# Layer norms applied behind the projections: a two-layer decoder step on one core

## The chip, the cores and the metric

The kernel runs on one core of a Trainium2 chip. The metric is the device time of one execution in microseconds. TensorE (PE) multiplies and writes its sums to PSUM; VectorE (DVE), ScalarE (ACT) and GpSimd (POOL) do the rest; each engine works off its own queue of instructions in order. SyncE (SP) only issues transfers. All arithmetic is float32: for the large products each operand is cut into two float32r parts.

## The reference, cut to what matters

The program is one inference step of a decoder with two layers, for 256 prompt tokens and 8 x 8 sample tokens (320 token columns), 2048 features, and a feed forward part 5504 wide:

```
for layer in (0, 1):
    x = LN(alpha * x + mixer(x))          # gamma, beta of ln_g[l, 0], ln_b[l, 0]
    x = LN(alpha * x + conv_ffn(x))       # gamma, beta of ln_g[l, 1], ln_b[l, 1]

conv_ffn(h):  gate, up = split(h @ w_up)
              out = (silu(causal_conv3(gate) + bias) * up) @ w_down
LN(x) = (x - mean) * rsqrt(var + eps) * gamma + beta     # over the 2048 features
```

There are four layer norms. After layer 0 the normalised x also feeds the keys and values (w_kv) and queries (w_q) of layer 1. The outputs are the last x, the new keys and values, and the last two gate rows of each sequence.

## The kernel before, in words

Activations are kept transposed: features on partitions, in 16 tiles of 128, and the 320 tokens on the free axis. `Stream` (L45) carries all weights, in chunks of up to 128 x 1024: SP loads a chunk (three buffers), ACT copies it to its high part (L82) and DVE subtracts for the low part (L84) into one of three `hl` buffers, and for each 128 x 128 tile of it PE does three matmuls over the 320 token columns (L123 to L125: high by high, high by low, low by high). A `Job` is one or more blocks of 256 columns of a weight matrix. When its sums are complete, `job.epi` takes them out of PSUM; `acc` has four buffers, a block needs two.

Everything else is a generator in `Lanes`, stepped after each half of a chunk. The tile framework then orders each engine's queue by its own estimate of when an operation is ready, program order being the priority; where `tc.keep_in_program_order` stands, the order is held.

`R` holds the residual stream. `epi_wo` and `epi_down` add products to it; with the last product of a tile, `ln_tile` adds to the sums `s1` (DVE) and `s2` (squares by ACT, sums by POOL). After the last tile `ln_end` has PE sum `s1` and `s2` over the partitions and DVE, ACT and PE turn these into mean and deviation (`ln_finish`, `spread`); `normalise` then takes POOL, DVE, ACT, ACT, DVE for each of the 16 tiles to make `xh` and `xl`, the two parts of the next projection's moving operand. The order is the same at three places, which this text calls A (after the mixer of layer 0, before its `up` jobs), B (after the feed forward of layer 0, before `kvb`) and C (after the mixer of layer 1). The fourth norm makes the output and has a path of its own (`out_end`).

`big` is a pool of four buffers for the arrays of 16 tiles. `ffn_consts` transposes gamma and beta into `lnp` and the conv's constants into `stc`; it starts as a lane at the fourth `wo` job. `gen_tables_b` (L592) builds a table for layer 1 on POOL; its lane is added when the feed forward of layer 0 begins, and in the profile it ran during the `wo` jobs ahead of A.

Of the kernel before, what the change touches and what calls it, by code (L numbers as in the profile page):

```python
# [18 lines left out]
NT = NPR + NSM  # L19
DM = 2048  # L20
KD = DM // 128
# [23 lines left out]
class Stream:  # L45
    """Weights in chunks: loaded, split into two float32r parts, multiplied, ahead of one another."""
# [57 lines left out]
    def run(self, job, steps, upto=None):  # L104
        """The job's chunks, all or those before upto; steps() after each half of one."""
        nc = self.nc
        accs = job.accs
        while self.done < (job.last if upto is None else job.first + upto):
# [8 lines left out]
            for (c, cw), acc in zip(tiles, accs[i]):  # L117
                for k in range(nk):
                    xh, xl = job.mv(k0 + k)
                    o = k * w + c  # L120
                    st, sp = k0 + k == 0, k0 + k == job.nk - 1
                    hi, lo = hl[:, 0, o:o + cw], hl[:, 1, o:o + cw]
                    nc.tensor.matmul(acc[:cw, :NT], hi, xh, start=st, stop=False)  # L123
                    nc.tensor.matmul(acc[:cw, :NT], hi, xl, start=False, stop=False)  # L124
                    nc.tensor.matmul(acc[:cw, :NT], lo, xh, start=False, stop=sp)  # L125
                    if self.fine and k == 1:
                        steps()
# [8 lines left out]
class Job:  # L136
    def __init__(self, w, cols, nk, mv, epi, k0=0, kc=4, on_pool=0):
        self.on_pool, self.accs = on_pool, {}
# [28 lines left out]
# the output's twelve chunks: 1 where ACT and Pool do the step, 0 where DVE does  # L167
# [9 lines left out]
def tile_yoco(  # L177
# [22 lines left out]
    def big(name, dt=F):  # L200
        return big_p.tile([128, 5120], dt, name=name, tag="big")
# [4 lines left out]
    def cols3(t):  # L206
        return t.rearrange("p (k n) -> p k n", n=NT)
# [27 lines left out]
    S = {"sel2": sel.rearrange("p j h q -> p j (h q)")}  # L235
    st = Stream(tc, raw_p, hl_p, acc_p, 3, 3)
# [8 lines left out]
    def mv_o(k):  # L245
        return S["oh"][:, k, :], S["ol"][:, k, :]
# [24 lines left out]
    def ffn_jobs(l):  # L271
        Wu, Wd = wview(ffn_w_up[l]), wview(ffn_w_down[l])

        def up(f0, n, wide):
            cols = []
            for a in range(0, n, 2):
                w = 128 * min(2, n - a)
                cols += [(128 * (f0 + a), w), (DFF + 128 * (f0 + a), w)]
            if wide:
                job(("up", l, f0, "w"), Wu, cols[:2], KD, mv_x, lambda i, t, f0=f0: epi_up(l, f0, i, t))  # L280
            for a in range(2 if wide else 0, len(cols), 2):
                for i in range(2):
                    job(("up", l, f0, a + i), Wu, [cols[a + i]], KD, mv_x,
                        lambda _, t, f=f0 + a, i=i: epi_up(l, f, i, t))
# [11 lines left out]
        for g, (f0, n) in enumerate(starts):  # L296
            if g == 0:
                up(f0, n, True)
            else:
                up(f0, 2, False)  # L300
                down(g - 1, *starts[g - 1])
                up(f0 + 2, n - 2, False)
# [11 lines left out]
    job("kvb", W_kv, [(0, 256), (256, 256)], KD, mv_x, lambda i, t: epi_kv("kb", i, t))  # L314
    for j in range(2):
        job(("vb", j), W_kv, [(512 + 256 * j, 256)], KD, mv_x, lambda i, t, j=j: epi_kv("vb", j, t))
    for hp in range(8):
        for g in range(3):
            job(("qb", hp, g), W_q, [(2048 * g + 256 * hp, 256)], KD, mv_x,
                lambda i, t, hp=hp, g=g: epi_qb(hp, g, t))  # L320
# [7 lines left out]
    def ln_prepare():  # L328
        """R becomes ALPHA * R less, for each token, the mean of its first 128 features."""
# [12 lines left out]

    def ln_tile(d):
        """The sums for one finished 128-feature tile of R."""
# [10 lines left out]
    def ln_end():  # L355
        """The last two tiles, and the means over all: tokens on partitions, 128 of them in each column."""
# [22 lines left out]
    def ln_finish(which, mode):  # L379
        """R becomes the normalised x; mode "xs" also stores it."""  # L380
        R, L, tk = S["R"], S["fp"], S["tk"]
        m, v, rs = tk[:, 0:3], tk[:, 4:7], tk[:, 8:11]

        def spread(x, name):
            """A column of tokens in each of three, to all partitions of a row."""
            p = ps(name)
            for t, n in TG:
                i = te.matmul(p[:, 128 * t:128 * t + n], x[:n, t:t + 1].to_broadcast([n, 128]), idf[:n, :n],
                              start=True, stop=True)
                tc.keep_in_program_order(i)  # L390
            o = L.tile([128, NT], F, name=name, tag=name)
            se.activation(out=o, in_=p[:, :NT], func=AF.Copy)
            return p[:, :NT], o

        pm, m1 = spread(m, "m1")
        ve.scalar_tensor_tensor(v, m, -1.0, m, OP.mult, OP.mult)
        ve.tensor_add(rs, S["pv"][:, 0:3], v)
        se.activation(out=rs, in_=rs, func=AF.Sqrt, bias=epst)
        ve.reciprocal(rs, rs)
        pr, rstd = spread(rs, "rstd")  # L400
        S["xh"] = cols3(big("xh", FR))
        S["xl"] = cols3(big("xl", FR))

        def normalise(d):
            r = R[:, d, :]
            if d < 2:
                ve.tensor_sub(r, r, pm)
            else:
                ge.tensor_sub(r, r, m1)
# [1305 lines left out]
```

## Time and profile before

| | |
|---|---|
| device time, median of 3 runs | 3329.16 us (3326.53 to 3330.91) |
| span of the profiled execution | 3326.8 us, 2.4 us below the median |
| PE busy | 3241.7 us, 97% |
| DVE, ACT, POOL busy | 1831.1, 1364.1, 625.1 us |
| mean granted TensorE clock | 0.982 of full |

The span runs from the first to the last instruction of one profiled execution; the device time contains it. Busy PE counts matmuls in flight, so it also counts matmuls that run at the lower clock.

### The profile page before, as it was taken

Reading aid. Unit: us, or ns where it says so; the run is one execution under the profiler, and the core shown is the slowest. Engines: PE = TensorE matmul, PEld = TensorE weight load, DVE = VectorE, ACT = ScalarE, POOL = GpSimd, SP = SyncE. Lnnn points to the kernel's source line nnn. Section 1 sums busy time; section 2 is a strip of 40 time slices with the busy share of each in tenths; the row PEclk is TensorE's granted clock in tenths of the full one; section 3 lists DMA queues with packets and bytes.
Section 4 is the critical chain, followed back from the end, with each engine's and each line's share of the span. In section 5 each row is a group of like instructions: output and inputs, shape, how many; then the busy total and the mean of one; then the engine's idle time right before and its main releaser. Section 6 shows DMA issues by size and latency. Waiting matters only on the chain.

```text
span 3326.8 us, 58327 instructions
## 1 busy us (share of the span) xinstructions
PE 3241.7 (97%) x23574; PEld 3053.7 (92%) x23574; DVE 1831.1 (55%) x3169; ACT 1364.1 (41%) x2209; POOL 625.1 (19%) x820
## 2 busy tenths in 40 slices
PE   9999999999999999999999999999999999999998
PEld 7789655989999999999899898878999999999998
DVE  5747644676555555555644444555665555555556
ACT  4643444344333333333544343343443333333333
POOL 2223543451000000000401111111210000000003
PEclk8999999989999999999899999999899999999998
DMA  6655787635444444444475767766354444444444
GB/s 187 148 187 152 251 295 282 165 113 156 149 152 148 151 152 148 152 149 149 133 247 157 216 186 206 209 196 182 103 157 151 148 152 149 150 153 147 151 151 139
DMA packets 543249, 562.75 MB, mean 169 GB/s; under 512 B 24598, under 2 KB 520926, under 8 KB 538806
## 3 DMA queue, kind: packets, MB, share of 16 engines
q1 hardware_dynamic: 520692, 468.87, 46.7%
q0 software_dynamic: 19856, 85.75, 7.6%
q10 hardware_dynamic: 2432, 4.40, 0.4%
q8 instruction: 186, 3.05, 0.4%
q14 instruction: 83, 0.68, 0.1%
HBM read 542.14 MB, written 17.59 MB: 168 GB/s over the span
## 4 chain that ended last, share of the span: by engine, by line
PE 90%; DVE 4%; DMA 3%; ACT 1%; issue 1%; POOL 0%; SPq 0%; DVEq 0%; ACTq 0%; POOLq 0%
PE acc L123 26%; PE acc L124 26%; PE acc L125 26%; PE kt L1258 1%; PE acc L1076 1%; DMA vtb<-in_cache_v_b_dram 1%; PE oa L1127 1%; PE s L1055 1%; PE s L1211 1%; PE s L1051 1%; DMA kx<-in_cache_kidx_a_dram,i 1%; PE s L1158 1%; PE ob L1301 1%; DVE R L410 1%; DVE hl L84 1%
## 5 line engine op out<-in xcount | busy, mean ns | idle before, releaser
L84 DVE TENSOR_TENSOR hl<-raw,hl 128x1024 fp32r<-128x1024 f32 (+1 forms) x752 | 928.3, 1235 | 870.5 <-ACT hl L82 867.0
L82 ACT ACTIVATE hl<-raw 128x1024 fp32r<-128x1024 f32 (+3 forms) x770 | 804.2, 1045 | 1314.6 <-PE acc L125 1112.6
L123 PE MATMUL acc<-xh,hl 128*128 128x320 f32 (+1 forms) x4176 | 1315.5, 315 | 6.6 <-ACT xh L412 5.1
L124 PE MATMUL acc<-xl,hl 128*128 128x320 f32 (+1 forms) x4176 | 1298.6, 311 | 7.2 <-DVE xl L414 7.2
L125 PE MATMUL acc<-xh,hl 128*128 128x320 f32 (+1 forms) x4176 | 1296.7, 311 | 1.5 <-POOL hl L84 1.1
L123 PEld LDWEIGHTS acc<-xh,hl 128*128 128x128 f32 (+1 forms) x4176 | 789.3, 189 | 31.1 <-issue 20.2
L124 PEld LDWEIGHTS acc<-xl,hl 128*128 128x128 f32 (+1 forms) x4176 | 788.5, 189 | 15.4 <-DVE xl L414 12.6
L125 PEld LDWEIGHTS acc<-xh,hl 128*128 128x128 f32 (+1 forms) x4176 | 788.0, 189 | 6.1 <-issue 3.5
L124 PE MATMUL acc<-H,hl 128*128 128x320 f32 x1376 | 425.4, 309 | 1.1 <-POOL H L568 1.1
L123 PE MATMUL acc<-H,hl 128*128 128x320 f32 x1376 | 426.0, 310 | 0.0
L125 PE MATMUL acc<-H,hl 128*128 128x320 f32 x1376 | 425.3, 309 | 0.3 <-DVE hl L84 0.3
L124 PEld LDWEIGHTS acc<-H,hl 128*128 128x128 f32 x1376 | 258.3, 188 | 1.6 <-POOL H L568 1.6
L125 PEld LDWEIGHTS acc<-H,hl 128*128 128x128 f32 x1376 | 258.3, 188 | 0.6 <-DVE hl L84 0.6
L123 PEld LDWEIGHTS acc<-H,hl 128*128 128x128 f32 x1376 | 258.2, 188 | 0.1
L586 DVE TENSOR_TENSOR R<-R,acc 128x320 f32<-128x320 f32 x352 | 169.7, 483 | 122.1 <-PE acc L125 121.8
L551 POOL COPY gl<-E 128x2 f32<-128x2 f32 x86 | 24.8, 288 | 1039.1 <-ACT E L547 1039.1
L568 POOL TENSOR_TENSOR H<-h,H 128x320 fp32r<-128x320 f32 x86 | 106.1, 1235 | 452.8 <-ACT H L567 438.6
L123 PE MATMUL acc<-oh,hl 128*128 128x320 f32 x512 | 161.9, 317 | 0.5 <-ACT oh L992 0.5
L124 PE MATMUL acc<-ol,hl 128*128 128x320 f32 x512 | 160.6, 314 | 0.9 <-DVE ol L993 0.9
L125 PE MATMUL acc<-oh,hl 128*128 128x320 f32 x512 | 160.3, 313 | 0.0
L1148 POOL TENSOR_TENSOR bm<-tt,pmb 128x256 f32<-128x256 f32 x48 | 45.4, 971 | 324.7 <-DVE mxb L941 309.4
L123 PEld LDWEIGHTS acc<-oh,hl 128*128 128x128 f32 x512 | 97.0, 190 | 2.8 <-ACT oh L992 1.2
(390 smaller groups left out, 3191.4 us busy)
## 6 DMA issues: line engine op xcount, KB each, us to landing
raw<-in_ffn_w_up_dram SPq DMA_DIRECT2D x336, 512.0 KB, 3.6
raw<-in_ffn_w_down_dram SPq DMA_DIRECT2D x160, 512.0 KB, 3.6
raw<-in_b_w_q_dram SPq DMA_DIRECT2D x96, 512.0 KB, 3.6
raw<-in_a_w_in_dram SPq DMA_DIRECT2D x64, 512.0 KB, 4.8
krb<-in_cache_k_b_dram SPq DMA_DIRECT2D x96, 256.0 KB, 3.6
vtb<-in_cache_v_b_dram SPq DMA_DIRECT2D x92, 256.0 KB, 5.6
raw<-in_a_w_o_dram SPq DMA_DIRECT2D x32, 512.0 KB, 4.3
raw<-in_b_w_o_dram SPq DMA_DIRECT2D x32, 512.0 KB, 5.0
```

What stands on the lines that cost most here:

```text
L82: a = self.nc.scalar.activation(out=hl[:, 0, :m], in_=raw[:, :m], func=AF.Copy)
L84: b = eng.tensor_sub(hl[:, 1, :m], raw[:, :m], hl[:, 0, :m].bitcast(F))
L123: nc.tensor.matmul(acc[:cw, :NT], hi, xh, start=st, stop=False)
L124: nc.tensor.matmul(acc[:cw, :NT], hi, xl, start=False, stop=False)
L125: nc.tensor.matmul(acc[:cw, :NT], lo, xh, start=False, stop=sp)
L410: ve.scalar_tensor_tensor(r, r, lnp[:, d, which:which + 1], pr if d < 2 else rstd, OP.mult, OP.mult)
L568: ge.tensor_sub(lo, h, hi.bitcast(F))
L586: ve.tensor_add(r, r, acc[:, :NT])
L1051: te.matmul(pv[:, :, 64 * hh:64 * hh + 64], S["sel2"][:, 8 * hh + b, :], S["ms"][:, 0:1024].rearrange("p (a t) -> p a t", t=16)[:, :, 4 * ...
L1055: te.matmul(p[32 * g:32 * g + 32, :], S["qsf"][:, b, 32 * g:32 * g + 32], kts[g], start=False, stop=True, tile_position=(0, 32 * g))
L1076: te.transpose(p[:, 128 * i:128 * i + 128], kr[:, o:o + 128], idf)
L1148: ge.tensor_add(bm[:, g, :], tt, S["pmb"][:, g, :])
```

## The change

At A, B and C the product is no longer taken with the normalised x. `epi_wo` and `epi_down` form gamma times the unnormalised row at once, in two parts: `scale_hi` (ACT) and `scale_lo` (DVE), into `rh` and `rl`. Two columns are added to each row, gamma and beta (`scale_gb`), so that a matmul moves 322 columns (`NX`) in all jobs whose operand is x: 172 blocks of 128 outputs in the two feed forwards and 56 in `kvb`, `vb` and `qb`. The extra columns give u = W gamma and v = W beta. `ln_stats` finds minus the mean and the inverse deviation meanwhile (`mr`). `fix` forms (acc + u * (-mean)) * rstd when a product leaves PSUM: one small ACT copy and two DVE operations of 320 columns for each block; v comes in as the bias or scalar of the operation behind it. `ln_rest` normalises R itself afterwards (POOL, DVE, ACT), since the residual is still needed.

At A and C `rl` takes the place of `ol`, the low part of the operand that the last `wo` job still reads: `gen_lo` writes it behind that job's chunks. The first part of `ffn_consts` (gamma and beta) now runs ahead of the first `wo` job of `mixer_end`. `gen_tables_b` is added at the first `down` job. The first `up` job is no longer two blocks wide.

```diff
@@ Stream.run
-                    nc.tensor.matmul(acc[:cw, :NT], hi, xh, start=st, stop=False)
+                    nx = job.nx
+                    nc.tensor.matmul(acc[:cw, :nx], hi, xh, start=st, stop=False)
...
+    def scale_hi(d):
+        se.activation(out=S["rh"][:, d, 0:NT], in_=S["R"][:, d, :], func=AF.Identity,
+                      scale=lnp[:, d, S["which"]:S["which"] + 1])
+    def scale_lo(d):
+        ve.scalar_tensor_tensor(S["rl"][:, d, 0:NT], S["R"][:, d, :], lnp[:, d, S["which"]:S["which"] + 1],
+                                S["rh"][:, d, 0:NT].bitcast(F), OP.mult, OP.subtract)
...
+    def ln_stats(mode=None):
+        yield
+        yield
...
+        for p, x in ((pm, S["s1"]), (pv, S["s2"])):
+            for t, n in TG:
+                te.matmul(p[:n, t:t + 1], x[:, 128 * t:128 * t + n], ones_d[:, 0:1], start=True, stop=True)
...
+        yield
+        yield
+        for k, x in enumerate((m, rs)):
+            p = ps("mr")
+            for t, n in TG:
+                te.matmul(p[:, 128 * t:128 * t + n], x[:n, t:t + 1].to_broadcast([n, 128]), idf[:n, :n],
+                          start=True, stop=True)
+            se.activation(out=S["mr"][:, k, :], in_=p[:, :NT], func=AF.Copy)
+        if mode:
+            S["norm"] = lanes.add(ln_rest(mode), 1.6)
...
+    def ln_rest(mode):
...
+            ge.tensor_add(r, r, S["mr"][:, 0, :])
+            ve.scalar_tensor_tensor(r, r, lnp[:, d, w:w + 1], S["mr"][:, 1, :], OP.mult, OP.mult)
+            se.activation(out=r, in_=r, func=AF.Identity, bias=lnp[:, d, 2 + w:3 + w])
...
+    def fix(acc, t):
+        if S["stats"] in lanes.lanes:
+            lanes.drain(S["stats"])
+        uv = const.tile([128, 2], F, name="uv", tag="uv", bufs=8)
+        se.activation(out=uv, in_=acc[:, NT:NX], func=AF.Copy)
+        ve.scalar_tensor_tensor(t, S["mr"][:, 0, :], uv[:, 0:1], acc[:, :NT], OP.mult, OP.add)
+        ve.tensor_mul(t, t, S["mr"][:, 1, :])
+        return uv[:, 1:2]
...
+    def gen_lo():
+        for d in range(0, KD, 4):
+            yield
+            if d == 12:
+                yield
+            scale_gb(d, 4)
+            for i in range(4):
+                scale_lo(d + i)
+            yield
@@ epi_wo
             ve.tensor_add(r, r, acc[:, :NT])
+            scale_hi(d)
@@ epi_up
+            x = Fp.tile([128, NT], F, name="fx", tag="fx", bufs=4)
+            v = fix(acc, x)
...
-                se.activation(out=e[:, 2:258], in_=acc[:, 0:256], func=AF.Copy)
+                se.activation(out=e[:, 2:258], in_=xp, func=AF.Identity, bias=v)
...
-                ve.tensor_mul(h[:, 0:256], c[:, 0:256], acc[:, 0:256])
+                ve.scalar_tensor_tensor(h[:, 0:256], xp, v, c[:, 0:256], OP.add, OP.mult)
@@ epi_down
+        if last and not l and p == 0:
+            S["which"] = 1
+            S["rh"], S["rl"] = cols3(big("rh", FR), NX), cols3(big("rl", FR), NX)
+            scale_gb(0, KD)
...
             ve.tensor_add(r, r, acc[:, :NT])
+            if last and not l:
+                scale_hi(d)
+                scale_lo(d)
@@ ffn
+        S["stats"] = lanes.add(ln_stats(), 1.0)
...
-        if l == 0:
-            lanes.add(gen_tables_b(), 0.5)
...
+                prep = lanes.add(chain(ln_rest("ffn"), ln_prepare()), 0.8)
+            if key[0] == "down" and key[2] == 0:
+                if prep in lanes.lanes:
+                    lanes.drain(prep)
+                if l == 0 and key[3] == 0:
+                    lanes.add(gen_tables_b(), 0.5)
@@ mixer_end
+        consts = ffn_consts(stn, lnn)
+        next(consts)
+        lanes.add(consts, 0.5)
         for p in range(8):
+            if p == 7:
+                lo = lanes.add(gen_lo(), 1.0)
             if ("wo", l, p) in jobs:
                 run(("wo", l, p))
-            if p == 3:
-                lanes.add(ffn_consts(stn, lnn), 0.5)
-        g = ln_finish(0, "ffn")
-        next(g)
-        lanes.add(g, 1.0)
+        lanes.drain(lo)
+        S["xh"], S["xl"] = S["rh"], S["rl"]
```

`epi_kv` (for `kb` and `vb`) and `epi_qb` call `fix` in the same way. The fourth norm keeps `ln_end` and `out_end`.

## Rows read from the trace of the kernel before

**Rows 1.** The page's part 1: busy time, share of the span, instructions.
```profile
span 3326.8 us, 58327 instructions
...
PE 3241.7 (97%) x23574; PEld 3053.7 (92%) x23574; DVE 1831.1 (55%) x3169; ACT 1364.1 (41%) x2209; POOL 625.1 (19%) x820
```

**Rows 2.** Waits on PE: waiting line <- releaser: total us, times, longest.
```profile
PE acc L124 <- DVE xl L414: 7.2, 6, 2.6
...
PE pm L371 <- DVE R L502: 2.6, 1, 2.6
...
PE acc L124 <- POOL H L568: 1.1, 1, 1.1
```

**Rows 3.** PE's matmuls into acc at A, B, C: stretch, length, busy (count), PEclk, DMA.
```profile
706.12:740.00 33.88, 17.05 (x82) 0.65 0.20 56
1638.95:1670.00 31.05, 18.38 (x100) 0.73 0.40 113
2373.51:2405.00 31.49, 20.65 (x104) 0.73 0.23 71
```

**Rows 4.** Timeline of PE at A: start, us, instruction, idle time before it.
```profile
720.05 1.44 PE L123 MATMUL acc<-xh,hl 128*128 128x320 f32 x4 [1.70 <-ACT xh L412]
721.28 1.27 PE L333 MATMUL shift<-R,ones_s 128*128 128x320 f32 x2
724.08 0.64 PE L124 MATMUL acc<-xl,hl 128*128 128x320 f32 x1 [1.53 <-DVE xl L414]
```

**Rows 5.** Timeline of PE at C: sums, then the spreading.
```profile
2373.95 0.81 PE L371 MATMUL pm<-ones_d,s 128*64 128x1 f32 x6
...
2376.91 1.07 PE L388 MATMUL m<-idf,tk 64*128 64x64 f32 x6
2377.91 1.63 PE L388 MATMUL rstd<-idf,tk 64*128 64x64 f32 x6
```

**Rows 6.** Timeline of PE: the first and last of 42 matmuls, 320 columns, kvb stage.
```profile
1702.18 0.31 PE L124 MATMUL acc<-xl,hl 128*128 128x320 f32 x1
...
1708.19 0.31 PE L123 MATMUL acc<-xh,hl 128*128 128x320 f32 x1
```

**Rows 7.** Timeline of PE: the first and last of eight matmuls, 256 columns, indexer.
```profile
105.49 0.28 PE L728 MATMUL is<-kitr,qh 128*128 128x256 f32 x1
...
106.31 0.28 PE L729 MATMUL is<-kitr,ql 128*128 128x256 f32 x1
```

**Rows 8.** PE's groups by line and shape: count, busy us, mean ns, idle before.
```profile
L123 PE MATMUL acc<-xh,hl 128*128 128x320 f32 x4160 | 1309.3, 315 | 5.4 <-ACT xh L412 5.1 <-issue 0.3
```

**Rows 9.** DVE by line: count, ns min/median/max.
```profile
L586 DVE TENSOR_TENSOR R<-R,acc x352: 471/481/489, 800.7 to 3300.3; 128x320 f32<-128x320 f32 x176
...
L410 DVE SCALAR_TENSOR_TENSOR R<-R,lnp,rstd x48: 537/546/1235, 718.9 to 2403.5; 128x320 f32<-128x320 f32 x48
```

**Rows 10.** All engines, last down group before B: length, PE, PEld, DVE, ACT, POOL.
```profile
1612.00:1640.00 28.00, 28.00 (x196) 27.87 (x194) 25.00 (x42) 14.61 (x26) 15.81 (x13) 1.00 0.56 173
```

**Rows 11.** POOL at 630 us and at C: table's load and user, then gamma's load.
```profile
630.24 0.50 POOL L600 DMA_DIRECT2D mk<-in_c_smaskb_dram  x1
...
634.06 1.08 POOL L602 TENSOR_TENSOR sb<-trb,mk 16x512 f32<-16x512 f32 x1 [1.08 <-DMA mk<-in_c_smaskb_dram]
...
2277.89 0.50 POOL L515 DMA_DIRECT2D lnn<-in_ln_b_dram  x1
```

**Rows 12.** Timeline of DVE: first sum of the mixer of layer 1.
```profile
2277.92 0.49 DVE L502 TENSOR_TENSOR R<-R,acc 128x320 f32<-128x320 f32 x1 [2.06 <-PE acc L125]
```

**Rows 13.** All engines in the feed forward of layer 0, columns as in rows 10.
```profile
800.00:900.00 100.00, 100.00 (x684) 100.00 (x683) 55.08 (x76) 38.30 (x51) 8.45 (x17) 1.00 0.50 154
```

**Rows 14.** POOL's work on the table sb: stretch, length, busy (count), PEclk, DMA.
```profile
610.00:715.00 105.00, 53.51 (x40) 0.97 0.51 153
```

**Rows 15.** Timeline of DVE: two splits during the table's making.
```profile
682.45 3.56 DVE L84 TENSOR_TENSOR hl<-raw,hl 128x1024 fp32r<-128x1024 f32 x1 [0.42 <-ACT hl L82]
686.33 1.22 DVE L84 TENSOR_TENSOR hl<-raw,hl 128x1024 fp32r<-128x1024 f32 x1 [0.32 <-ACT hl L82]
```

More of the change, by code (lines that the diff above doesn't have):

```diff
@@ new lines, in ln_rest @@
+    def ln_rest(mode):
+        R, w = S["R"], S["which"]
+        for d in range(KD):
+            r = R[:, d, :]
+            ge.tensor_add(r, r, S["mr"][:, 0, :])
+            ve.scalar_tensor_tensor(r, r, lnp[:, d, w:w + 1], S["mr"][:, 1, :], OP.mult, OP.mult)
+            se.activation(out=r, in_=r, func=AF.Identity, bias=lnp[:, d, 2 + w:3 + w])
+            if mode == "xs" and d % 4 == 3:
+                a = d - 3
+                sy.dma_start(out=xs[1][:, a * NT:(a + 4) * NT], in_=R[:, a:a + 4, :].rearrange("p k n -> p (k n)"))
+            yield
@@ L377, in ln_end @@
         st.pin = 1
[L379 to L409, printed above, removed]
-            ve.scalar_tensor_tensor(r, r, lnp[:, d, which:which + 1], pr if d < 2 else rstd, OP.mult, OP.mult)
-            bias = lnp[:, d, 2 + which:3 + which]
-            se.activation(out=S["xh"][:, d, :], in_=r, func=AF.Identity, bias=bias)
-            se.activation(out=r, in_=r, func=AF.Identity, bias=bias)
-            ve.tensor_sub(S["xl"][:, d, :], r, S["xh"][:, d, :].bitcast(F))
-            if mode == "xs" and d % 4 == 3:
-                a = d - 3
-                sy.dma_start(out=xs[1][:, a * NT:(a + 4) * NT], in_=R[:, a:a + 4, :].rearrange("p k n -> p (k n)"))
-        for d in range(KD):
-            normalise(d)
-            if d >= 3:
-                yield
     def out_prepare():
@@ L489, in out_end, with ln_pair @@
             rest[n]()
-    def ln_pair(p):
-        if p == 7:
+    def ln_pair(p, out=False):
+        if p == 7 and out:
             ln_end()
@@ L512, in ffn_begin @@
         ge.dma_start(out=stn[19:20], in_=ffn_conv_b[l:l + 1])
-        lnn = Fp.tile([4, DM], F, name="lnn", tag="lnn")
+        lnn = Fp.tile([16, TRW], F, name="lnn", tag="trb")[0:4, 0:DM]
         ge.dma_start(out=lnn[0:2], in_=ln_g[l])
@@ L648, in ffn @@
             return
-        g = ln_finish(1, mode)
-        next(g)
-        return g
+        S["xh"], S["xl"] = S["rh"], S["rl"]
+        S["stats"] = lanes.add(ln_stats("xs"), 1.0)
+        return True
     def epi_ki(accs):
@@ L904, in epi_kv @@
                 t = S["kvp"].tile([128, n], F, name="vt", tag=tag, bufs=bufs)[:, :NT]
-            se.activation(out=t, in_=acc[:, :NT], func=AF.Copy)
+            if kind in ("k", "v"):
+                se.activation(out=t, in_=acc[:, :NT], func=AF.Copy)
+            else:
+                x = S["lnpool"].tile([128, NT], F, name="fx", tag=("sh", "s1", "s2")[kv % 3])
+                v = fix(acc, x)
+                se.activation(out=t, in_=x, func=AF.Identity, bias=v)
             lanes.add(gen_kv(kind, kv, t), 1.0)
@@ L1178, in epi_qb @@
             h = 2 * hp + i
-            se.activation(out=S["qbp"][hp % 2][:, i, g, :], in_=acc[:, 0:256], func=AF.Copy)
-            ve.tensor_copy(S["qbs", hp // 2][:, g, :, h % 4, :], acc[:, 256:320].rearrange("p (b q) -> p b q", q=8))
+            x = S["lnpool"].tile([128, NT], F, name="fx", tag=("sh", "s1", "s2")[(6 * hp + 2 * g + i) % 3])
+            v = fix(acc, x)
+            se.activation(out=S["qbp"][hp % 2][:, i, g, :], in_=x[:, 0:256], func=AF.Identity, bias=v)
+            ve.tensor_scalar(S["qbs", hp // 2][:, g, :, h % 4, :], x[:, 256:320].rearrange("p (b q) -> p b q", q=8),
+                             v, None, OP.add)
     KVB = {"k": cache_k_b, "v": cache_v_b}
```

97 lines of the change are left out of this document (59 added, 38 removed).

## The prediction

> **What bounds the kernel now.** I read the page's busy times first: PE is busy for 3241.7 of 3326.8 us, 97%, and DVE for 55% [rows 1]. So the kernel is a stream of matmuls, and a change is worth what it takes from or adds to that stream. The view of waits on PE then gives little: 7.2 us for the low part that `normalise` makes, 2.6 for R, 1.1 for the last H [rows 2]. That understates the norms, because PE's busy time also counts matmuls in flight and matmuls at half clock. So I compared time with matmuls done. The measure is the spacing of starts in the stream: 42 matmuls of 320 columns from 1702.18 to 1708.19 us make 41 steps, 0.1466 us each [rows 6].
>
> At A, from the last `wo` matmul to 740 us, 82 matmuls into acc are done in 33.88 us; at 0.1466 they need 12.0, so 21.9 are lost. At B 100 in 31.05 us need 14.7: lost 16.4. At C 104 in 31.49 us need 15.2: lost 16.2. Sum 54.5 us, and the granted clock in these stretches is 0.65 to 0.73 [rows 3]: PE first waits for sums and deviation, then for the parts tile by tile [rows 4], and part of this passes at the lower level of 1.2 GHz. The 54.5 us contain both the waiting and the lower clock.
>
> **The change part by part.** *The stalls go.* At A and C the first chunk of `up` needs tiles 0 to 3 of `rh` and `rl`, which are made before the last `wo` block ends; at B likewise behind the last `down` blocks. I take all 54.5 us away and put back what PE must still do in the stream.
>
> *What PE keeps.* The 12 matmuls that sum `s1` and `s2` and 12 that spread the result stay. At full clock 24 of the first kind took 2.96 us, from 2373.95 to 2376.91, so 12 take 1.5; six of the second took 1.00, to 2377.91, so 12 take 2.0 [rows 5]. That is 3.5 us at each place, 10.5 in all. The two matmuls of the shift ran inside the gap at A, 1.27 us at half clock [rows 4], and the same two sit in the gap at C; in the full stream they cost about half of that, 0.7 at each of A and C, 1.4. The gaps are then worth 54.5 - 10.5 - 1.4 = 42.6 us.
>
> *Two more columns.* 172 blocks in the feed forwards and 56 in layer 1's projections make 228 blocks of 16 x 3 matmuls: 10944. (Line 123 alone runs 4160 times with x [rows 8]: 228 x 16 and 512 of layer 0's projections.) The price of a column: 256 columns take 0.82 us for seven steps, 0.117 each [rows 7], and 320 take 0.1466 [rows 6]; 64 columns differ by 0.0295 us, 0.46 ns each, and 0.1466 / 320 is 0.458 as well. So there is no fixed part, and two columns cost 0.916 ns: 10.0 us. From below, one column at full clock of 2.4 GHz is 0.417 ns, 9.1 us. From above I leave open a charge in steps, since 256 and 320 are both multiples of 64; it is a rival. I take 10.0.
>
> *DVE at B.* In the last `down` group DVE was busy for 25.0 of 28.0 us [rows 10], eight blocks of 3.5 us. `scale_lo` adds two operations a block, 0.48 to 0.55 us each [rows 9], 8 to 9 us in all, so DVE ends up to 6 us behind. The `hl` buffers hold two chunks, 7 us of lead, and the next chunks need only early tiles. Bounds 0 and 9; I take 4. Behind DVE wait the freeing of acc and the next splits.
>
> *Gamma and beta earlier.* At C the loads of `lnn` are issued on POOL until 2278.4 us [rows 11], while the first sum of that mixer is ready at 2277.9 [rows 12]. A load on this queue took 3.3 us from the end of its issue to its user's start (630.74 to 634.06) [rows 11]. So the transposes can't run before about 2281.7. If PE's queue holds them too early, PE waits up to 4 us, and ACT with `scale_hi`, the split of the next chunk behind it. The lead of two chunks covers most. Bounds 0 and 4; I take 1.5 at C and 0.5 at A, where the first sum comes some 14 us after the loads: 2.
>
> *Late statistics.* The sums of squares end on POOL; PE's six plus six matmuls stand in its queue where the framework expects them ready. At A the old ones waited 2.6 us for R [rows 2]. Bounds 0 and 3 a place; I take 0.5, 1.5 in all.
>
> *The last H of a layer.* PE waited 1.1 us for it [rows 2]; `fix` puts an ACT copy and a DVE multiply, about 1 us, ahead of it, in both layers: 2.
>
> *Costed at nothing.* `fix` itself, 228 times two DVE operations of 0.48 to 0.55 us [rows 9], some 235 us of DVE: in the feed forward a block pair of gate and up comes every 21 us, so it raises DVE from 55 to about 65 of 100 us [rows 13], and acc has a whole further pair of buffers for the 3.5 to 14 us that the next job takes. Without that cover each block would cost 1 us. `ln_rest` does what `normalise` did, in a stretch where DVE was full and PE ran on; `scale_hi` and the small copies lie on ACT, 38 of 100 us [rows 13]. The tiles that `gen_lo` can only write after the last `wo` matmul are four DVE operations, 2.2 us, and the fourth `up` chunk that needs them comes 10.6 us later. The one-block `up` job changes only the order. SP's queue moves no weight load; the store of x after B is issued a little later than now and is read only by the mixer of layer 1.
>
> Sum: -42.6 + 10.0 + 4 + 2 + 1.5 + 2 = -23.1 us. Span 3326.8 becomes 3303.7; the median lies 2.4 above the span, so 3306.
>
> **The table moved.** `gen_tables_b` kept POOL busy for 53.5 us beside the `wo` jobs [rows 14], and DVE's split took 3.56 us next to it instead of 1.22 [rows 15]. It now runs in the feed forward, where DVE has 35 of 100 us free after `fix` [rows 13]. If POOL's work stretches DVE's by its own length, 53.5 us over some 150 us still fit, and I cost it at nothing. The Trainium skill, "GPSIMD Engine Reference", Key points, says that GpSimd shares its SBUF interfaces with VectorE, with contention for DVE instructions that have two SBUF inputs. The splits of rows 15 agree. Its page "SBUF — State Buffer", Who interferes with whom, goes further and calls it an exclusive lock: by that the loser stands still, as the third rival has it.
>
> **The rivals.** *Columns charged in steps.* If a row of 322 columns is charged like 336, each matmul costs 7.3 ns (16 x 0.458) instead of 0.9: 80 us instead of 10, hence 3376, slower. For it: no matmul of before has a width that is not a multiple of 64 in this mode, and rows now start every 1288 bytes instead of every 1280. Against: the cost is proportional down to 256 [rows 6, 7]. It decides from 3.0 ns a matmul, (23 + 10) us / 10944, some seven columns. A step of four (324) would give 3316.
>
> *The gap comes back smaller.* DVE behind at B by the full 9 us, PE held by `lnn` and the sums at their upper bounds (4 at each of A and C, 3 at each place) would add 5 + 6 + 7.5 = 18.5: 3324.5, within 0.2%. For it: DVE is nearly full before B [rows 10]. Against: each term has two chunks of lead.
>
> *POOL blocks DVE.* If all of the table's 53.5 us stop DVE at a time when the lane of `ln_rest` or the conv needs it, PE loses what DVE cannot make up. With 35 us free in 100 and the table packed into 100 us, 18.5 remain: 3324.5; with the whole of it lost, 3359. Against: the table's loads and stores space it out, 53.5 in 105 us [rows 14].
>
> *The stalls stay.* The framework could place the statistics so that PE waits for them as before. Then only the columns are left: 3339, slower. Against: the first product needs them only after its 96 matmuls, 14 us.
>
> **How the numbers follow.** Two runs of this kernel tell apart about 0.2%, 6.7 us. The forecast: 0.72, own range 3294 to 3318 (terms at their lower bounds give 3306 - 9.5 - 0.9 = 3296; the upper side takes half of the bounds and a step of four). The smaller gap: 0.10, half of it faster than 3322.5. Columns in large steps: 0.08. POOL: 0.06, half of it faster, the rest same or slower. Stalls that stay: 0.04. Faster: 0.72 + 0.05 + 0.03 and part of the rest, 0.82; same 0.08; slower 0.10. The predicted time is 3306 us; 3293 to 3323 leaves out 2 in 10.
>
> **What would show it.** In the profile after: matmuls of 322 columns spaced 0.1475 us (0.154 would mean the large steps); at A, B and C the clock at 1.00 throughout, and 82, 100 and 104 matmuls in 16 to 21 us; no wait of PE for a low part; waits of PE for `pm`, `lnp` or `hl` of at most a few us each; DVE at 65 of 100 us in the feed forward. The prediction is wrong if the spacing exceeds 0.149 us, if PE's clock still falls at one of the three places, or if PE waits for DVE's splits around the table or at B for over 10 us.

## The result, and the profile after

The changed kernel is slower: 3371.7 us (median of 4 runs, 3367.3 to 3374.0) against 3328.9 for the kernel before (4 runs, 3326.5 to 3330.9), a ratio of 1.0131 with a 95% interval of 1.0117 to 1.0145. The profiled execution has a span of 3371.3 us, 44.5 more than before; the forecast was 23.1 less. The page after, part 1:

```profile
span 3371.3 us, 58900 instructions
...
PE 3253.3 (96%) x23526; PEld 3063.3 (91%) x23526; DVE 2089.3 (62%) x3655; ACT 1413.5 (42%) x2434; POOL 710.1 (21%) x832
```

PE is busy 11.6 of the 44.5 us longer than in [rows 1], and idle for the rest. The view of waits on PE, after, whole span:

```profile
PE acc L127 <- DVE hl L85: 16.6, 9, 3.6
PE acc L125 <- ACT hl L83: 11.0, 2, 9.9
PE acc L125 <- DVE R L535: 8.1, 1, 8.1
...
PE acc L125 <- DVE R L629: 6.2, 5, 1.5
```

The waits for `xl` and `xh` of [rows 2, 4] are gone, and of those for the sums 2.1 us are left. New ones stand in their place: 27.6 us for the split weights (`hl`) of ACT and DVE, 8.1 us for R in the `wo` stage, and 6.2 us for R in the last `down` group and just behind it. In the kernel before, the same waits for splits came to 2.0 us:

```profile
PE acc L123 <- ACT hl L82: 1.2, 1, 1.2
...
PE acc L125 <- DVE hl L84: 0.8, 2, 0.4
```

The windows at A, B and C, matmuls into acc, cut after the last block as in [rows 3] (length, busy and count, PEclk, DMA):

```profile
716.87:750.75 33.88, 24.35 (x148) 0.95 0.30 89
1656.74:1687.79 31.05, 14.21 (x78) 0.85 0.36 111
2415.84:2447.33 31.49, 26.10 (x172) 1.00 0.28 84
```

At A and C PE does 148 and 172 matmuls where it did 82 and 104; at B it does 78 where it did 100. To see where that comes back I cut both traces into stages at the starts of the matmuls into acc (us from first to last start; a gap is the step between two stages; "first 480" are the `up` jobs ahead of the first `down`; groups of 96 and 192 run to the start of the matmul behind them). The last three columns are kernels of the experiments below: m1 is the change with the table moved by a named order; k1 also has the shift put first and `ln_rest` spread out; k4 also has rows 324 apart, and at B fewer low parts in the group and the additions on DVE.

| stage | before | after | m1 | k1 | k4 |
|---|---|---|---|---|---|
| `wo`, layer 0 | 121.7 | 131.3 | 127.7 | 119.7 | 119.1 |
| gap A | 14.1 | 0.1 | 0.1 | 0.1 | 0.1 |
| first 480 behind A | 78.5 | 88.1 | 81.1 | 77.2 | 77.1 |
| rest of feed forward 0 | 809.5 | 816.0 | 816.0 | 816.0 | 813.9 |
| its last `down` group | 30.3 | 35.2 | 35.1 | 35.2 | 31.0 |
| gap B | 9.9 | 1.5 | 1.5 | 1.5 | 0.4 |
| `kvb` to `qb`, layer 1 | 553.5 | 581.6 | 578.9 | 566.3 | 559.3 |
| its first 96 matmuls | 21.1 | 37.4 | 37.4 | 24.1 | 20.6 |
| `wo`, layer 1 | 170.5 | 175.3 | 175.0 | 172.2 | 171.3 |
| gap C | 7.9 | 0.1 | 0.1 | 0.1 | 0.1 |
| first 480 behind C | 79.2 | 82.0 | 82.0 | 77.1 | 77.0 |
| rest of feed forward 1 | 809.5 | 815.5 | 815.5 | 815.5 | 813.9 |

The gaps close as forecast: 31.9 us become 1.7. But 9.6 us come back in `wo`, 9.6 in the first 480 behind A, 16.3 in the first 96 behind B, and 2.8 behind C, and the undisturbed stretches are 6.5 and 6.0 us longer. The indexing stage ahead of all this took from 322.4 to 332.5 us in the kernels of this study (322.4 to 329.7 in those that leave it as it was). So differences of a few us in a whole time are not read below; stages are.

Three places of the trace after show how it comes back. *In `wo`*, the timeline of PE (start, us, instruction, idle time before it and releaser):

```profile
617.74 1.15 PE L561 MATMUL lnp<-idf,lnn 4*128 4x4 f32 x16
618.82 0.81 PE L331 MATMUL shift<-R,ones_s 128*128 128x320 f32 x2
...
630.44 0.61 PE L125 MATMUL acc<-oh,hl 128*128 128x320 f32 x1 [8.05 <-DVE R L535]
```

The transposes of gamma and beta, now at the start of the mixer's end, stand ahead of the mixer's shift in PE's queue. In the kernel before, that shift ran ahead of the first `wo` matmul:

```profile
583.42 0.71 PE L333 MATMUL shift<-R,ones_s 128*128 128x320 f32 x2
```

The scaling of R needs the shift's product, so the first sum of R is late, its acc buffer is not freed, and PE waits 8.05 us.

*At B*, the timeline of ACT:

```profile
1675.44 0.56 ACT L394 ACTIVATE R<-R,lnp 128x320 f32<-128x320 f32 x1 [0.93 <-DVE R L393]
1676.51 0.56 ACT L394 ACTIVATE R<-R,lnp 128x320 f32<-128x320 f32 x1 [0.51 <-DVE R L393]
...
1682.92 0.56 ACT L394 ACTIVATE R<-R,lnp 128x320 f32<-128x320 f32 x1 [0.51 <-DVE R L393]
1683.39 1.04 ACT L83 ACTIVATE hl<-raw 128x1024 fp32r<-128x1024 f32 x1
```

Eight activations of `ln_rest` come every 1.07 us, about the pace of POOL's additions (sixteen in 16.42 us), and the next split of weights stands behind them: the 9.9 us.

*At A*, POOL still makes the table, though the diff adds that lane only at the first `down`. POOL, then DVE:

```profile
702.83 3.17 POOL L649 TENSOR_TENSOR sb<-trb,mk 16x1024 f32<-16x1024 f32 x1
...
714.56 3.13 POOL L649 TENSOR_TENSOR sb<-trb,mk 16x1024 f32<-16x1024 f32 x1
```

```profile
703.13 0.47 DVE L535 TENSOR_TENSOR R<-R,acc 128x320 f32<-128x320 f32 x1
703.64 2.71 DVE L419 TENSOR_TENSOR s<-s,R 128x320 f32<-128x320 f32 x1
...
712.43 5.61 DVE L347 SCALAR_TENSOR_TENSOR ol<-R,lnp,rh 128x320 fp32r<-128x320 f32 x4
```

All of the table's operations run from 623.6 to 719.6 us, beside `wo` as in the kernel before (618.6 to 710.9). I read this as the framework's estimate: it had the table's inputs ready in `wo` and put POOL's instructions there, wherever the lane was added. Four `scale_lo` took 5.61 us beside it instead of the 2 us of [rows 9].

### The profile page after: what moved, and what is told of

The parts are those of the page before. It is cut to its first block, busy times and chain, and to the rows that moved or that the text cites. A ratio compares the mean times of both kernels' runs of the same rounds, so it can differ in the third digit from the quotient of the medians.

```text
span 3371.3 us, 58900 instructions
## 1 busy us (share of the span) xinstructions
PE 3253.3 (96%) x23526; PEld 3063.3 (91%) x23526; DVE 2089.3 (62%) x3655; ACT 1413.5 (42%) x2434; POOL 710.1 (21%) x832
## 4 chain that ended last, share of the span: by engine, by line
PE 45%; DVE 3%; DMA 1%; issue 1%; ACT 0%; SPq 0%; POOL 0%; DVEq 0%; ACTq 0%; POOLq 0%
PE acc L125 14%; PE acc L127 13%; PE acc L126 13%; PE kt L1316 1%; PE s L1269 1%; DMA vtb<-in_cache_v_b_dram 1%; PE ob L1359 1%; DVE hl L85 1%; DVE R L393 1%; PE s L1213 1%; DMA krb<-in_cache_k_b_dram 0%; DVE s L419 0%; PE s L1212 0%; DVE rl L347 0%; DVE R L629 0%
## 5 line engine op out<-in xcount | busy, mean ns | idle before, releaser
L125 PE MATMUL acc<-rh,hl 128*128 128x322 f32 x3648 | 1155.0, 317 | 12.5 <-ACT hl L83 9.9
L127 PE MATMUL acc<-rh,hl 128*128 128x322 f32 x3648 | 1136.8, 312 | 16.2 <-DVE hl L85 16.2
L126 PE MATMUL acc<-ol,hl 128*128 128x322 f32 (+1 forms) x3264 | 1018.2, 312 | 0.9 <-DVE ol L1048 0.9
L125 PEld LDWEIGHTS acc<-rh,hl 128*128 128x128 f32 x3648 | 690.6, 189 | 25.8 <-issue 14.5
L127 PEld LDWEIGHTS acc<-rh,hl 128*128 128x128 f32 x3648 | 690.6, 189 | 21.1 <-DVE hl L85 18.6
L126 PEld LDWEIGHTS acc<-ol,hl 128*128 128x128 f32 x3264 | 621.2, 190 | 2.9 <-issue 1.2
L126 PE MATMUL acc<-rl,hl 128*128 128x322 f32 x896 | 281.0, 314 | 0.0
L126 PEld LDWEIGHTS acc<-rl,hl 128*128 128x128 f32 x896 | 171.4, 191 | 1.9 <-issue 1.2
L125 PE MATMUL acc<-oh,hl 128*128 128x320 f32 x512 | 162.3, 318 | 9.2 <-DVE R L535 8.1
L125 PE MATMUL acc<-xh,hl 128*128 128x320 f32 (+1 forms) x528 | 169.5, 321 | 1.5 <-ACT hl L83 1.2
L127 PE MATMUL acc<-xh,hl 128*128 128x320 f32 (+1 forms) x528 | 164.2, 311 | 1.5 <-POOL hl L85 1.1
```

Source lines behind the costliest of these rows:

```text
L125: nc.tensor.matmul(acc[:cw, :nx], hi, xh, start=st, stop=False)
L126: nc.tensor.matmul(acc[:cw, :nx], hi, xl, start=False, stop=False)
L127: nc.tensor.matmul(acc[:cw, :nx], lo, xh, start=False, stop=sp)
```

## The experiments

The theory: two more columns cost about twice the forecast, and the rest of the loss is queue order and POOL's load beside DVE, at the places shown. Rivals: columns in large steps; the amount of work that the change adds to DVE, in whatever order. "Before" in a ratio is the kernel before on the same chip.

### What a column costs

The kernel before with only the columns or the row length of x changed:

```diff
-    big_p.tile([128, 5120])   S["xh"] = cols3(big("xh", FR))
+    big_p.tile([128, KD * NS])   S["xh"] = cols3(big("xh", FR), NS)
-    nc.tensor.matmul(acc[:cw, :NT], hi, xh, ...)
+    nc.tensor.matmul(acc[:cw, :nx], hi, xh[:, :nx], ...)   # nx = NX in up, kvb, vb, qb
+NS, NX = 322, 322   # e1;   322, 320   # e2;   324, 322   # e3
```

> The kernel before with nothing of the change but its columns: 322 columns from rows 322 elements apart in the same 10,944 matmuls (the two extra columns hold copies of constants and nothing reads them). Theory: these matmuls alone cost what their mean spacing in the changed kernel shows, 0.1484 against 0.1466 us, 1.75 ns each: plus 19 us, about 3348. Rival, the prediction's term: two columns at the measured price of a column, plus 10 us, 3339. Rival, columns charged in blocks of 16: plus 80 us, 3409.

> The kernel before with 320 columns, but rows 322 elements apart, so that seven of eight rows begin at another place of their 64 bytes. Theory: in the changed kernel the odd rows, which begin 8 bytes off a multiple of 16, show about 1 ns more than the even ones; where a row begins is then part of the cost, and this kernel loses about 9 us (3338) with no column added. Rival: only the count of columns costs; then no change (within 3 us of 3329).

> 322 columns as in the first experiment, but rows 324 elements apart, so that every row begins at a multiple of 16 bytes (one small constant load of the tables is single-buffered to make room). Theory: only the two columns are left to pay, plus 10 us (3339) or a little under. Rival, where a row begins does not matter: as the first experiment, plus 19 us (3348).

Measured: e1 3348.2 us, ratio 1.0056 (1.0039 to 1.0073); e2 3334.1, 1.0013 (1.0002 to 1.0024); e3 3347.8, 1.0050 (1.0034 to 1.0066). Two starts 41 steps apart in the timeline of PE, e1, e2, e3 in turn, to be read as [rows 6]:

```profile
1733.41 0.31 PE L125 MATMUL acc<-xh,hl 128*128 128x322 f32 x1
...
1739.49 0.31 PE L127 MATMUL acc<-xh,hl 128*128 128x322 f32 x1
```

```profile
1674.10 0.31 PE L127 MATMUL acc<-xh,hl 128*128 128x320 f32 x1
...
1680.13 0.31 PE L126 MATMUL acc<-xl,hl 128*128 128x320 f32 x1
```

```profile
1683.95 0.31 PE L127 MATMUL acc<-xh,hl 128*128 128x322 f32 x1
...
1690.00 0.31 PE L126 MATMUL acc<-xl,hl 128*128 128x322 f32 x1
```

6.08, 6.03 and 6.05 us for 41 steps, against 6.01 before. The mean over the 3638 steps between neighbouring x matmuls in the rest of a feed forward, where PE waits for nothing, is sharper (layer 0, layer 1): 0.14667 and 0.14667 us before, 0.14849 and 0.14833 in e1, 0.14738 and 0.14722 in e2, 0.14792 and 0.14792 in e3, and after as in e1. So with rows that begin at multiples of 16 bytes the two columns cost 1.26 ns, 13.7 us over 10,944 matmuls; rows 322 apart cost another 0.4 to 0.7 ns, 4 to 8 us, with or without the columns. Together that is 18 to 20 us, and e1 as a whole lost 19.4. The large steps (7.3 ns a matmul) are refuted. E2 lost 5 us, not the 9 that I had read from odd and even rows. The whole time of e3 does not show its gain, its interval reaches from 11 to 22 us; that rests on the spacing, and on the rest of the feed forward, 813.9 us against e1's 816.0. Part of the gain is lost again in the indexing stage, where PE waits 2.8 us for the load that became single-buffered (5.0 in g6, 5.1 in h4).

### The shift ahead of the transposes

```diff
-    lanes.add(mixer_begin(0), 1.0)
+    first = mixer_begin(0)
+    next(first)
+    next(first)
+    lanes.add(first, 1.0)
```

> The changed kernel with one edit: the first two steps of the shift of the first layer's R are issued before the transposes of the norm's constants, so that they no longer stand behind them in PE's queue. Theory: PE's wait of 8.1 us for the first R add of the wo stage goes, and with it some slow clock: 8 to 11 us less than the changed kernel, 3361 to 3364. Rival: R's scaling was held by DVE beside the table on POOL, which stays: then the wait stays at over 5 us and the time within 3 us of 3372.

3367.7 us, 1.0115 (1.0095 to 1.0136); span 3359.4. That is 4 us less than the change by the medians and 12 by the spans, where I expected 8 to 11. The wait is gone and `wo` takes 121.6 us, 9.7 less. The first 480 took 90.9, 2.8 more: part of it is given back at once. My reading, which no run tests, is that what follows was no more ready than before.

### Holding the order by hand

G2 acts at B alone, g3 at all three norms (with the shift first, and the table held behind `ln_rest` on POOL); g5 and g6 also move low parts of R out of the last `down` group.

```diff
     def ln_rest(mode):
-            ge.tensor_add(...)   ve.scalar_tensor_tensor(...)   se.activation(...)
+            for x in (ge.tensor_add(...), ve.scalar_tensor_tensor(...), se.activation(...)):
+                tc.keep_in_program_order(x)
+            st.pin = max(st.pin, 3)          # and the next three splits; g2: mode "xs" only
-                sy.dma_start(out=xs[1]...)
+                se.dma_start(out=xs[1]...)
-            S["norm"] = lanes.add(ln_rest(mode), 1.6)
+            S["norm"] = lanes.add(ln_rest(mode), 0.5)      # and no drain of it in begin_b
# g3:
+        with tc.issue_after(S["rest_end"].ins):
             ge.dma_start(out=tr, in_=trd)
# g5, g6, in epi_down; the other twelve in a lane of the next projection:
-                scale_lo(d)
+                if p % 2 and i: scale_lo(p // 2)
# g6: NS = NT + 4 for the rows of rh, rl, oh, ol
```

> The changed kernel with one edit at the norm after the first feed forward: the rest of the norm (ln_rest) is stepped at 0.5, its three operations and the next splits are held in the order written, its stores go behind the activations on ScalarE's queue, and the second layer's buffers do not wait for it. Theory: the 9.9 us that PE waits for ScalarE's split and the waits behind it come from eight activations of ln_rest, paced by POOL, ahead of the split: 12 to 15 us less than the changed kernel, 3357 to 3360. Rival: DVE, full with the splits of R, is late there anyway: the wait turns up on DVE's splits and at most 4 us are gained, 3368 or more.

> The changed kernel with the shift first, ln_rest and the next splits held in the order written behind all three norms, and the second layer's table held behind the last addition of ln_rest on POOL. Theory: every loss beyond the matmuls' own is the order of the queues and the table's load: the waits on splits in the first up jobs (10 us behind the first norm, 5 behind the third) and the 9.9 us go too, 33 to 38 us less than the changed kernel, 3334 to 3339. Rival: DVE is too full with what the change added there, in whatever order: the waits move to its own operations, and the time stays over 3346.

> As g3_all_held, and twelve of the sixteen low parts of R in the last down group are made in the first four chunks of the next projection, four in the group. Theory: the group's 4.9 us come from DVE's 16 more operations of 0.48 us; 3 to 5 us less than g3_all_held. Rival: the same operations are then late for the projection: no gain, the group shorter and the first chunks longer by as much.

> As g5_lo_later, with rows 324 elements apart, so that every row begins at a multiple of 16 bytes. Theory: the mean spacing of the 322-column matmuls falls from 0.1483 to 0.1477 us as between the first and the third experiment, 6 us less than g5_lo_later over 10,944 of them, some 3326 to 3330, level with the kernel before. Rival: the spacing is hidden by other waits there; no gain.

G2: 3366.2 us, 1.0103 (1.0083 to 1.0123), where I expected 3357 to 3360. The first 96 matmuls behind B fell from 37.4 to 24.5, so these 12.9 us were the order; but the fifth 96 took 19.0 instead of 15.2, and over `kvb` to `qb` 8.8 us remain of the gain. G3: 3378.4, 1.0147 (1.0125 to 1.0169), slower than the change itself; my number was 40 us off. Its waits on PE from 700 to 830 us:

```profile
PE acc L125 <- ACT hl L83: 9.2, 2, 5.6
PE acc L127 <- DVE hl L85: 4.2, 4, 2.9
```

A split that is held stands behind every activation issued so far, those of `epi_up` among them, which wait for DVE's `fix`. The wait for ACT moved from B to A and C: the first 480 took 97.3 and 92.9. G5 (3380.3, 1.0144) shortened the group from 35.2 to 31.0, and lost more than that behind it (`kvb` to `qb` 578.6 against 570.5), as its rival said. G6 (3379.3, 1.0139, span 3368.2) is within the noise of g5. So "hold everything" was a wrong cure, and it left open whether the order or the load on DVE was to blame.

### The table, and the price of the rest of the norm

H1 holds only the table (and has the shift first). N1 is h1 without the arithmetic of `ln_rest`. H3 spreads `ln_rest` and leaves the splits free; h4 is h3 with rows 324 apart.

```diff
# h3: add n, scale n - 2, bias n - 3 in one step
+        for n in range(KD + 3):
+            if n < KD: S["rest_end"] = ge.tensor_add(...)          # tile n
+            if 0 <= n - 2 < KD: pin(ve.scalar_tensor_tensor(...))  # tile n - 2
+            if n >= 3: pin(se.activation(...))                     # tile n - 3
+            yield
# n1, from h1
-            S["rest_end"] = ge.tensor_add(...)   ve.scalar_tensor_tensor(...)   se.activation(...)
+            if d == 0: S["rest_end"] = ge.tensor_add(...)
```

> The changed kernel with the shift first and the second layer's table held on POOL behind the last addition of ln_rest; nothing else is held. In g3_all_held the wo stage of layer 0 fell to 119.7 us (131.3 in the changed kernel, 121.6 with the shift first), but the first 480 matmuls of the next stage took 97.3 (88.1; 90.9 with the shift first). Theory: the splits held there behind the epilogues' activations were to blame, and the table beside DVE takes its part: wo stage near 120, the 480 matmuls 84 to 88. Rival: the table costs nothing there, and they stay at 90 or more.

> As h1_table_held, and ln_rest issued in three stages (POOL's addition two steps ahead of DVE's scaling, this one step ahead of ScalarE's bias), DVE's and ScalarE's parts held behind what is already issued, the splits free; stores on ScalarE's queue, 0.6 a step at the second norm, and the second layer's buffers do not wait for it. Theory: a split then never stands behind an operation of ln_rest that waits for another engine: the first 480 matmuls behind the first norm take 80 to 84 us, the first 96 behind the second 22 to 25, and the time is 3335 to 3345. Rival: DVE's amount of work there, not its order, is the bound: 88 or more for the 480, and 3355 or more.

> As h3_rest_spread, with rows 324 elements apart. Theory: 6 us less than h3_rest_spread, by the spacing, which puts it near the kernel before (3329 to 3339). Rival: no gain.

> As h1_table_held with ln_rest left out but for one addition: R keeps the unnormalised rows, so the residual path of what follows is another; the projections and their corrections are as in the change. It prices the moved rest of the norm. Theory: nearly all that the first jobs lose beyond their columns is ln_rest: the 480 matmuls behind the first norm take 80 us or less, the first 96 behind the second 23 or less, 25 us less than h1_table_held in all. Rival: the corrections of the products (two more operations on DVE and one on ScalarE for each tile) are the load: the 480 matmuls stay over 85 us.

H1: 3371.3, 1.0134 (1.0117 to 1.0151); `wo` took 119.7 as expected, but the 480 behind A 91.7, as the rival said, and the first `down` jobs behind them 28.6 instead of 21.0. H3: 3354.9, 1.0081 (1.0064 to 1.0098), over the 3335 to 3345 expected. H4: 3350.7, 1.0075 (1.0058 to 1.0092), not told from h3. N1: 3344.6, 1.0054 (1.0037 to 1.0070). N1 against h1 prices `ln_rest` as h1 has it: 27 us by the medians, 34 by the spans. (In n1 the table starts 21 us earlier, so at A the price is not of `ln_rest` alone; `kvb` to `qb` and the 480 behind C, where there is no table, fell by 11.1 and 5.8.) Spreading `ln_rest` gave h3 what I expected behind B (24.0 for the first 96) and brought the 480 behind C to 77.1, less than in the kernel before, but behind A they still took 89.5, and n1, without the work, 83.5. What A has and C has not is the table, which h1, h3 and n1 let start right behind `ln_rest`. H3 around A, POOL and then DVE:

```profile
719.95 18.26 POOL L398 TENSOR_TENSOR R<-R,sel 128x320 f32<-128x320 f32 x16 [8.82 <-ACT sel L382]
...
744.04 3.10 POOL L663 TENSOR_TENSOR sb<-trb,mk 16x1024 f32<-16x1024 f32 x1
```

```profile
717.81 1.23 DVE L85 TENSOR_TENSOR hl<-raw,hl 128x1024 fp32r<-128x1024 f32 x1 [1.75 <-ACT hl L83]
...
723.36 1.88 DVE L85 TENSOR_TENSOR hl<-raw,hl 128x1024 fp32r<-128x1024 f32 x1 [2.81 <-ACT hl L83]
725.17 0.53 DVE L419 SCALAR_TENSOR_TENSOR fx<-sel,uv,acc 128x320 f32<-128x320 f32 x1
...
736.32 1.16 DVE L402 SCALAR_TENSOR_TENSOR R<-R,lnp,sel 128x320 f32<-128x320 f32 x1
...
744.34 3.15 DVE L402 SCALAR_TENSOR_TENSOR R<-R,lnp,sel 128x320 f32<-128x320 f32 x1
```

The same split takes 1.23 us alone and 1.88 beside POOL's sixteen additions; the same scaling takes 0.54 alone, 1.16 beside the additions and 3.15 beside one operation of the table, with which it ends (747.14 and 747.49). The operation at 725.17, whose second tensor is in PSUM, takes its usual time beside the additions. (Not every two-input operation waits: one of `fix` at 727.85 took 0.49.) The Trainium skill, "SBUF — State Buffer", Who interferes with whom, says that a DVE instruction with two SBUF inputs contends with a GpSimd instruction that reads SBUF, that this is an exclusive lock, and that a DVE instruction with at most one SBUF input, outside its 2-port modes, does not contend. The rows shown agree with it; the operation of 0.49 us shows no such wait.

### The table late

Pieces of the table go to the later groups of feed forward 0, each behind an earlier POOL instruction there. N2 is k1 without the arithmetic of `ln_rest`, c1 is the kernel before with the table late, m1 the changed kernel with nothing but the table late.

```diff
-                if l == 0 and key[3] == 0:
-                    lanes.add(gen_tables_b(), 0.5)
+            if l == 0 and key[0] == "down" and key[2] == 1 and key[3] == 0:
+                lanes.add(gen_tables_b(), 0.25)
         # in gen_tables_b, for the load of tr and for each mk
+        with tc.issue_after(S["pool_op"].ins):       # a copy of epi_up
# k3, in epi_down: eight low parts in the group, eight in a lane of the next projection
-                scale_lo(d)
+                if i: scale_lo(p)
# k4: ln_rest "xs" six steps later, rate 0.9, its addition on DVE
-                ge.tensor_add(r, r, S["mr"][:, 0, :])
+                pin(ve.tensor_add(r, r, S["mr"][:, 0, :]))
```

> As h3_rest_spread, with the second layer's table made piece by piece in the later groups of the first feed forward, behind the norm's rest and away from it. In h3_rest_spread DVE's operations behind the first norm lasted 1.16 us beside POOL's additions and 3.15 us beside the table's, 0.54 alone. Theory: this contention is what keeps the first 480 matmuls at 89.5 us there, where the third norm, without the table, has 77.1: they fall to 79 to 82 and the time by 8 to 11 us, to 3344 to 3347. Rival: the number of DVE's operations is the bound: the 480 stay at 87 or more.

> As k1_table_late with all of ln_rest's arithmetic left out (R keeps the unnormalised rows). It prices what ln_rest costs when it is spread and without the table beside it. Theory: most of its price was order and contention, so little is left: 6 to 12 us less than k1_table_late. What this kernel still has over the one before is then the price of the columns (19 us) and of the corrections, less the gaps closed. Rival: its 48 operations cost by their number: 20 us or more less.

> Control: the kernel before, with the table in the later groups as in k1_table_late and nothing else. Theory: in the kernel before, the table lies beside wo with DVE idle enough; its place matters little, within 4 us of the kernel before. Rival: the table stretches the first norm's chain there as well; 5 us or more are gained, and the change has to be held against that.

> The changed kernel with one edit, the second layer's table made in the later groups of the first feed forward; shift, ln_rest and splits as in the change. It separates the table from the spreading of ln_rest. Theory, contention and order add up: the 480 matmuls behind the first norm fall from 88.1 to 78 to 81 us, the wo stage by 1 or 2 (its wait for the shift stays), the second norm stays as it is: 3360 to 3364. Rival: without the spreading, ln_rest alone holds the splits: 85 us or more for the 480, and no gain beyond 3 us.

> As k1_table_late, with rows 324 elements apart, and half of the low parts of R in the last down group made in the next projection's first four chunks, with the splits free. Theory: 4 to 6 us by the spacing, 3 to 4 by the group (35.2 to 32 us, the first chunks no longer): 3334 to 3340. Rival: the low parts are late for the projection as in g5_lo_later, and only the spacing is gained, 3339 to 3342.

> As k3_late_324_lo, and at the second norm ln_rest begins six steps later and does its additions on DVE, not POOL. In k3 DVE's split beside POOL's sixteen additions lasted 1.9 us (1.23 alone), and the first 192 matmuls of the projection took 42.7 us (35.8 in the kernel before). Theory: without POOL beside them they take 36 to 39, 4 to 6 us less than k3_late_324_lo, 3319 to 3321, which is below the kernel before by 0.15 to 0.2%. Rival: the 16 additions cost DVE as much as the contention did: the same as k3.

K1: 3328.2 us, 1.0006 (0.9997 to 1.0016), 27 us less than h3 where I expected 8 to 11: the 480 behind A fell from 89.5 to 77.2 as the theory had it, and the first `down` jobs behind them from 31.5 to 21.0, which I had not counted. The waits on PE from 700 to 800 us, k1:

```profile
PE acc L127 <- DVE hl L85: 1.4, 2, 0.7
```

N2: 3321.8, 0.9990 (0.9979 to 1.0000). Spread and away from the table, `ln_rest` costs 3 us by the spans (3323.1 against 3325.9) and 6 by the medians, not 27 to 34: its price was order and contention, not its 48 operations. K1 does all of the change's work and is level with the kernel before, so the rival of the amount of work falls. C1: 3323.0, 0.9997 (0.9986 to 1.0008): no gain that can be told in the kernel before, though its gap at A shrank from 14.1 to 9.3. M1: 3356.9, 1.0078 (1.0065 to 1.0091), some 15 us less than the change: behind A the 480 fell to 81.1, B is as it was (37.4). The rest of feed forward 0, where the table now lies, stays at 816.0. So table and order add up.

K3: 3325.1, 1.0003 (0.9994 to 1.0013). Group and gap at B gave 5.2 us, the second 96 of the projection took 21.8 instead of 15.9; in whole time it is not told from k1. K4: 3317.8, 0.9962 (0.9949 to 0.9974), faster than the kernel before, and beyond what c1 allows for the table's place alone. DVE behind B, k3 with POOL's additions beside it, then k4 without:

```profile
1651.72 1.89 DVE L86 TENSOR_TENSOR hl<-raw,hl 128x1024 fp32r<-128x1024 f32 x1
```

```profile
1650.13 1.22 DVE L86 TENSOR_TENSOR hl<-raw,hl 128x1024 fp32r<-128x1024 f32 x1
```

The first 192 matmuls took 35.6 us (k3 42.7, before 35.8). K4's windows, cut as in [rows 3]:

```profile
709.44:743.32 33.88, 30.77 (x207) 1.00 0.33 96
1632.11:1663.16 31.05, 25.83 (x167) 1.00 0.79 227
2363.92:2395.41 31.49, 28.39 (x191) 1.00 0.31 92
```

207, 167 and 191 matmuls where the kernel before has 82, 100 and 104, at full clock. This is what the forecast described for the change as written.

## Why the prediction was wrong

*The stalls go*: right. 31.9 us of gaps became 1.7, and no wait for `xl` is left. But the 54.5 us were to be given back only by the sums, the spreading and the shift. That failed at three steps which I costed at nothing or at 0.5 us, and a fourth was too small. Of the signs that I had named, the clock fell to 0.85 at B and 0.95 at A, and PE waited 7.8 us for DVE's splits behind A and 3.6 behind B; the spacing stayed under 0.149.

*`ln_rest` "in a stretch where DVE was full and PE ran on"*: the step that failed most. Its 48 operations cost 27 to 34 us where they were put (n1 against h1), because each waits for another engine inside a queue that also carries the splits. I had looked at the work alone, which does cost only 3 to 6 us (n2 against k1), and not at what stands behind it.

*The table moved, "I cost it at nothing"*: it was not moved into the feed forward at all. The framework left it beside `wo`, and there DVE had gained `scale_lo` and the splits of the first `up` jobs. M1, which does move it, is 15 us faster, and there the price of nothing holds: the rest of the feed forward is no longer for it. My rival "POOL blocks DVE" had the mechanism, with a chance of 0.06, but was priced by the idle share of the feed forward; there, without the table, DVE has 67.4 of 100 us (forecast 65).

*Gamma and beta, 0.5 us at A, bounded by 4*: PE waited 8.05 us. I followed the late load to ACT and DVE, and did not ask what else stood behind the transposes on PE. It was the mixer's shift, which no term has (the shift of 1.4 us is that of the feed forward); putting it first takes 9.7 us from the `wo` stage (f1). *Late statistics, 1.5 us*: about right, PE waits 2.1.

*Two more columns, 10.0 us*: mis-sized. 13.7 for the columns and some 6 for rows 1288 bytes apart, 18 to 20 together. My upper bound went to large steps, which do not exist here; the row length stood in the rival's sentence and had no price of its own.

*DVE at B, 4 us*: the group lost 4.9, and g5 and k3 show that the low parts are the cause. *`fix` at nothing*: right in the feed forwards, whose rest is 6.5 and 6.0 us longer, which is 3648 matmuls times the spacing's 1.7 to 1.8 ns. *The last H, 1 us in each layer*: the last group of layer 1 is 0.9 longer.

Added up from the stages, the gaps give 30.2 us back. `wo` of layer 0 takes 9.6, the 480 behind A 9.6, the 96 behind B 16.3, the group before it 4.9, the 480 behind C 2.8, the columns elsewhere some 17, the last group of layer 1 0.9: 61.1, a net loss of 31. The other 13 of the 44.5 us lie in the attention part of layer 1 (7), in `wo` of layer 1 (4.8) and in single us. I have no test of these, and their cause stays open. The `wo` of layer 1 took 170.5 to 175.5 us in all these kernels, c1 among them with 173.0, so I don't put it down to the change. Of the 7 us, k1 and n2 still show some 5 when the first 96 and the columns are taken off, so neither the table nor the placing of `ln_rest` explains them.

## What to carry to other kernels

Work taken off the critical path must still be put somewhere: when a gap is filled, look at what stands behind each moved instruction in its queue, and behind what it waits for, rather than at its busy time. Where a framework orders the queues, a lane that is added later in the code need not be later on the chip: here the table stayed where it was until an instruction was named that it must follow; and holding everything in order (g3) can be worse than holding only the moved work and leaving the urgent instructions free (h3, k1). A mean that says DVE has a third of its time free says nothing about the 20 us in which POOL runs beside it.

## What the runs showed of the hardware

Two float32r columns more than 320 cost 0.63 ns each with rows 1296 bytes apart (e3), against 0.46 for a column below 320, and rows of the moving operand 1288 bytes apart cost 0.6 to 0.7 ns a matmul by themselves (e2). Why is not settled by these runs: the mean steps of the 16 tiles of x scatter from 145.6 to 151.0 ns in the trace after and as widely in e3, where every row begins at a multiple of 16 bytes.

In h3 the 48 scalings of `ln_rest` on DVE, with both tensors in SBUF, took from 0.53 to 3.16 us, the longest of them beside POOL's table. The 228 first operations of `fix`, with one tensor in PSUM, all took 0.53 to 0.55.
